# A transformer block in fp32 on one core: every SBUF tile gets another address

## The chip, the core and the metric

The kernel runs on one core of one Trainium2 chip. The time is that of the device, in microseconds; three runs of the kernel before gave 1016.59, 1017.27 and 1018.25 us (median 1017.27). The core's engines are TensorE (PE; its weight loads are listed as PEld), VectorE (DVE), ScalarE (ACT), GpSimd (POOL) and SyncE (SP), which here issues nearly all DMAs. SBUF is the core's working memory: 128 partitions, and every tile occupies the same byte range in each of them. Addresses below are such byte offsets within a partition, in units of 1024 bytes (K).

## The reference

One layer of a Conformer macaron block on 512 tokens of width 1024, in fp32:

```python
x = x + 0.5 * swiglu(rmsnorm(x, ffn1_norm), w_gate1, w_up1, w_down1)   # D_FF = 2816
proj = rmsnorm(x, mix_norm) @ w_in
out_a = chunked_relbias_attention(qa, ka, va, a_rel_bias)              # 8 heads of 64
out_b = mla_attention(c_q, c_kv, k_rope, ...)                          # 8 heads, q and k of 96
x = x + concatenate([out_a, out_b]) @ w_out
x = x + 0.5 * swiglu(rmsnorm(x, ffn2_norm), w_gate2, w_up2, w_down2)
x = rmsnorm(x, final_norm)

def swiglu(h, w_gate, w_up, w_down):
    return (silu(h @ w_gate) * (h @ w_up)) @ w_down
```

## The kernel before

Activations are held transposed, model or hidden dimension on the partitions and the 512 tokens along the row, so one tile of 128 rows by 512 fp32 takes 2K. Precision comes from splitting: each operand is a high part and a low part, and `mm3` (L150 to L153) makes each product of three matmuls: moving high on weights high, moving high on weights low, and moving low on weights high (their lines in the trace are L151, L153 and L152). A matmul of 512 columns has one stationary operand (128 by 128, loaded by a PEld instruction) and one moving operand of 512 columns, both read from SBUF.

The stages on PE, in order:

- FFN 1, gate and up (`gu`): for each of 22 hidden tiles two outputs of 8 x 3 matmuls, 1056 in all. Stationary: the split weights `whi`, `wlo`. Moving: the split input `xh`, `xl`.
- FFN 1, down (`dn`): 8 output tiles of 22 x 3 matmuls, 528 in all. Moving: the split hidden tiles `h1h`, `h1l`.
- Mixer: input projections (`pj`; here the weights move and `xh`, `xl` are stationary), then the attention of 16 heads.
- Output projection (`wo`, 192 matmuls; moving: `xh`, `xl`, which now hold the attention's output).
- FFN 2, gate and up (1056; moving: `x2h`, `x2l`), and down (moving: `h2h`, `h2l` for the first 14 hidden tiles, and `xh`, `xl`, used again, for the last 8). The last output tile is done in two halves of 256 columns.

`wunit` (L137 to L148) prepares weights: a DMA brings a block of 128 x 1024 into `raw`, ACT writes `whi` (L146) and POOL or DVE writes `wlo` (L147), four buffers each. `gate` (L156 to L168) makes a hidden tile from two finished PSUM banks on DVE, ACT and POOL.

The order on the engines comes from the recording layer's scheduler. The places of the tiles come from pools, which are stacked in the order of their opening: `const` (with `x`, `xh`, `xl`), `wpool` (`raw`, `whi`, `wlo`), `work`, `small`, and above them in turn the pools of the stages, `h1`, `mix` and `h2`, which use one range one after the other. A tile of a later stage waits until the instructions that use an older tile in its range are through. The addresses before, from the built program:

| tiles | before |
|---|---|
| x | 16.1K to 32.1K |
| xh, xl | 32.1K to 64.1K |
| raw | 69.4K to 85.4K |
| whi, wlo | 85.4K to 117.4K |
| work, small | 117.4K to 129.8K |
| h1h, h1l in turn | 129.8K to 217.8K |
| x2h, x2l, then h2h, h2l in turn | 129.8K to 217.8K |

In bytes, each tile of xh and xl begins 128 past a multiple of 512, each block of whi and wlo 384 past one, each tile of the h1 and h2 pools 256 past one.

Of the kernel before, what the change touches and what calls it, by code (L numbers as in the profile page):

```python
# [32 lines left out]
# columns of the packed parameter array  # L33
# [6 lines left out]
def tile_macaron_block(  # L40
# [20 lines left out]
    const = ctx.enter_context(tc.tile_pool(name="const", bufs=1))  # L61
    wpool = ctx.enter_context(tc.tile_pool(name="wpool", bufs=4))
    work = ctx.enter_context(tc.tile_pool(name="work", bufs=2))
    small = ctx.enter_context(tc.tile_pool(name="small", bufs=2))

# [1 line left out]
    x = [const.tile([P, S], F32, name=f"x{k}") for k in range(KD)]  # L67
    XH = [const.tile([P, S], F32R, name=f"xh{k}") for k in range(KD)]
    XL = [const.tile([P, S], F32R, name=f"xl{k}") for k in range(KD)]
    col = const.tile([P, NCOL], F32, name="col")  # L70
    raw0 = [wpool.tile([P, 1024], F32, tag="raw", name="raw") for _ in range(2)]
# [41 lines left out]
    def rsqrt(out, v, y, y2):  # L113
        """out = v^-1/2: by logarithm and exponential, then one Newton step."""
        act.activation(y, v, AF.Ln)
        act.activation(y, y, AF.Exp, scale=-0.5)
        dve.tensor_tensor(out=y2, in0=y, in1=y, op=ALU.mult)
        dve.tensor_tensor(out=y2, in0=y2, in1=v, op=ALU.mult)
        dve.tensor_scalar(out=y2, in0=y2, scalar1=-0.5, scalar2=1.5, op0=ALU.mult, op1=ALU.add)
        dve.tensor_tensor(out=out, in0=y, in1=y2, op=ALU.mult)  # L120

    def rstd_rows(ps):
        """rs[:, n] = (mean_d x[d, n]^2 + eps)^-1/2 on every partition."""
        sh = work.tile([P, S], F32R, tag="wa", name="sh")
        sl = work.tile([P, S], F32R, tag="wa", name="sl")
        act.copy(sh, ssum)
        dve.tensor_tensor(out=sl, in0=ssum, in1=sh.bitcast(F32), op=ALU.subtract)
        m = ps.tile([P, S], F32, tag="mm", name="ms")
        pe.matmul(m, lhsT=ones, rhs=sh, start=True, stop=False)
        pe.matmul(m, lhsT=ones, rhs=sl, start=False, stop=True)  # L130
        v = work.tile([P, S], F32, tag="wb", name="v")
        y = work.tile([P, S], F32, tag="wa", name="y")
        y2 = work.tile([P, S], F32, tag="wc", name="y2")
        dve.tensor_scalar(out=v, in0=m, scalar1=EPS, scalar2=None, op0=ALU.add)
        rsqrt(rs, v, y, y2)

    def wunit(src, n, lo_on=None, raw=None, step=1024):  # L137
        """A block of weights, split: hi + lo, both exact in 12 bits."""
        if raw is None:
            raw = wpool.tile([P, 1024], F32, tag="raw", name="raw")  # L140
            nc.sync.dma_start(out=raw[:, :n], in_=src)
        hi = wpool.tile([P, 1024], F32R, tag="whi", name="whi")
        lo = wpool.tile([P, 1024], F32R, tag="wlo", name="wlo")
        for c in range(0, n, step):
            cc = slice(c, min(n, c + step))
            act.copy(hi[:, cc], raw[:, cc])  # L146
            (lo_on or pool).tensor_tensor(out=lo[:, cc], in0=raw[:, cc], in1=hi[:, cc].bitcast(F32), op=ALU.subtract)  # L147
        return hi, lo  # L148
# [6 lines left out]
    def ffn(ps, gu, dn, H, XH, XL, after, raw0=None, squares=None, last=None):  # L155
        def gate(f, gup):  # L156
            """h = silu(g) u = (g / 2) (tanh(g / 2) + 1) u, split."""
            gs = work.tile([P, S], F32, tag="wa", name="gs")
            th = work.tile([P, S], F32, tag="wb", name="th")
            us = work.tile([P, S], F32, tag="wc", name="us")  # L160
            hh, hl = H[f]
            dve.tensor_tensor(out=gs, in0=gup[0], in1=rs, op=ALU.mult)  # L162
            act.activation(th, gs, AF.Tanh, scale=0.5)  # L163
            dve.scalar_tensor_tensor(out=us, in0=gup[1], scalar=0.5, in1=rs, op0=ALU.mult, op1=ALU.mult)  # L164
            dve.scalar_tensor_tensor(out=gs, in0=th, scalar=1.0, in1=gs, op0=ALU.add, op1=ALU.mult)  # L165
            pool.tensor_tensor(out=us, in0=us, in1=gs, op=ALU.mult)  # L166
            act.copy(hh, us)
            pool.tensor_tensor(out=hl, in0=us, in1=hh.bitcast(F32), op=ALU.subtract)  # L168
# [45 lines left out]
    # =====================================================  FFN 1  # L214
    with tc.tile_pool(name="h1", bufs=1, reuse_waits="tile") as hp, \
            tc.tile_pool(name="ps1", bufs=8, space=PSUM, reuse_waits="tile") as ps:
        H = [(hp.tile([P, S], F32R, name=f"h1h{f}"), hp.tile([P, S], F32R, name=f"h1l{f}")) for f in range(NF)]
        # the tensor engine's clock rises while the first loads are under way
        warm = ps.tile([P, S], F32, tag="mm", name="warm")
        dve.memset(H[0][0].bitcast(F32), 0.0)  # L220
        for _ in range(9):
            pe.matmul(warm, lhsT=H[0][0][:, 0:P], rhs=H[0][0], start=True, stop=True)

        for k in range(KD):
            split_x(k, C_FFN1)

        def squares():
            for k in range(KD):
                add_square(k, True)

        def after1(dt):
            split_x(dt, C_MIX)
            add_square(dt)

        ffn(ps, gu1, dn1, H, XH, XL, after1, raw0, squares)

    # =====================================================  mixer
    AH, AL = XH, XL
    with tc.tile_pool(name="mix", bufs=1, reuse_waits="tile") as mp:
        qA = mp.tile([P, NT, 512], F32, tag="qA", name="qA")  # L240
        kA = mp.tile([P, NT, 512], F32, tag="kA", name="kA")
        lat = mp.tile([P, NT, LAT], F32, tag="qB", name="lat")
        latT = mp.tile([P, 6, S], F32R, tag="vAh", name="latT")
        kB = mp.tile([P, NT, 512], F32, tag="kB", name="kB")
        VBh = mp.tile([P, NT, 4, 192], F32R, tag="vBh", name="VBh")
        VBl = mp.tile([P, NT, 4, 192], F32R, tag="vBl", name="VBl")
# [8 lines left out]
        # rtab[:, q/k, t, :]: cos*g1, sin*g2, sin*g1, cos*g2  # L255
# [11 lines left out]
        def factors(ss, n, width, scaled, name):  # L267
            """ss [P, NT, n] sums of squares -> factors of the RMS norm, rtok folded in where scaled."""
# [13 lines left out]
        def rope(dst, src, fac, i, n, tmp):  # L282
            """src [P, NT, n, 32] * fac -> normalised, rotated, into dst (gains in rtab)."""
# [13 lines left out]
        with tc.tile_pool(name="ps2", bufs=1, space=PSUM, reuse_waits="tile") as ps:  # L297
            NB = {"s": 2, "tr": 2, "t": 3, "pv": 1}

            def bank(group, i, name):  # L300
                """Bank i of one of the two groups of four."""
                tag = (("s",) * NB["s"] + ("tr",) * NB["tr"], ("t",) * NB["t"] + ("pv",) * NB["pv"])[group][i]
                return ps.tile([P, 512], F32, tag=tag, name=name, bufs=NB[tag])

            def in_proj(off, n, group):
                """The columns off.. of W_in for all tokens: four banks, one per token tile."""
# [10 lines left out]
            def sumsq(src, ss, nh, width):  # L317
                """ss[.., h] = sum of squares over each group of width columns of src."""
# [5 lines left out]
            # latents, with the token statistics  # L324
# [46 lines left out]
            # B: queries from their latents  # L371
# [25 lines left out]
            # B: keys and values from their latents  # L397
# [29 lines left out]
            def values_proj():  # L427
                """A: values."""
# [15 lines left out]
            def transposes(src):  # L444
                """The four token tiles of src(t) [128, n], transposed into one bank [n, 512]."""
# [13 lines left out]
            def front(h):  # L459
                """Transposed, scaled and split queries and keys of a head (A: of its pair)."""  # L460
# [37 lines left out]
            def softmax(qh, ql, kh, kl, bias):  # L498
                """Probabilities of the query tiles 3..0, on 128 (i + 1) keys each."""
                pa = wpool.tile([P, 1024], F32, tag="raw", name="pa")  # L500
                pb = wpool.tile([P, 1024], F32, tag="raw", name="pb")
# [18 lines left out]
            def flip(pi):  # L520
                """Probabilities with the keys on the partitions, split: keys 0 | keys 1 and keys 2 | keys 3."""
# [34 lines left out]
            # the stages of four neighbouring heads overlap  # L556
# [14 lines left out]
    # =====================================================  output projection, FFN 2, final norm  # L571
    with tc.tile_pool(name="h2", bufs=1, reuse_waits="tile") as hp, \
# [3 lines left out]
        H = [(hp.tile([P, S], F32R, name=f"h2h{f}"), hp.tile([P, S], F32R, name=f"h2l{f}")) for f in range(14)]  # L576
# [18 lines left out]
        # final norm: per half of the tokens, rstd as columns, spread over the partitions by the tensor engine  # L595
# [11 lines left out]
        def means(h):  # L607
            """The mean squares of these tokens in columns, with the last tile's part."""
# [46 lines left out]
def _kxm(w, kt, m):  # L655
    """[kt*128, m] -> [128, kt, m]: the rows of each k tile on the partitions."""
    return w.reshape(kt, P, m).transpose(1, 0, 2)
# [10 lines left out]
def _layout(i):  # L668
# [17 lines left out]
    # the bias of query p and key column c of a tile whose last 128 columns are the query's own block  # L686
# [34 lines left out]
```

## Time and profile before

| | before |
|---|---|
| three runs | 1016.59, 1017.27, 1018.25 us |
| profiled execution: span of its instructions (its whole time is not listed apart) | 1016.7 us |
| PE busy | 993.1 us, 98% |
| PE weight loads | 813.7 us, 80% |
| POOL, DVE, ACT busy | 591.5, 397.3, 387.6 us |
| HBM read | 87.02 MB, 88 GB/s over the span with the writes |

Matmuls overlap in this trace: one is listed with some 0.39 us from its start to its end, while the next starts after some 0.23 us. So the busy share says little of PE's pace; the distance from one matmul's start to the next one's, the pitch, says it. The profiled span lies 0.6 us below the median of the runs.

### The profile page before, as it was taken

The numbers are of one execution on the slowest core, as the hardware profiler recorded it, in microseconds if no ns is written. First come the engines' busy times: TensorE is split into PE (matmuls) and PEld (weight loads), VectorE is DVE, ScalarE is ACT, GpSimd is POOL, SyncE is SP. The second block draws the span as 40 slices with busy tenths as digits, with TensorE's granted clock in tenths as the row PEclk, the third lists the DMA queues.
The fourth block names the chain that finished last, engine by engine and source line by source line (L and its number), as shares of the span: only waits on it lengthen the run. The fifth ranks groups of instructions, "written<-read, shape, count | busy, mean of one in ns | idle before, by whom it ended". The sixth has DMA issues, their size and how long they took to land.

```text
span 1016.7 us, 12060 instructions
## 1 busy us (share of the span) xinstructions
PE 993.1 (98%) x4579; PEld 813.7 (80%) x4579; DVE 397.3 (39%) x687; ACT 387.6 (38%) x648; POOL 591.5 (58%) x429
## 2 busy tenths in 40 slices
PE   7999999999999999898999999999999999999996
PEld 4888888888888889786778978888888888888886
DVE  7534324323121224776788845143333332200002
ACT  4433323323222225663678853343232332222220
POOL 7586676676555521285355567586666656645540
PEclk7999999999999999998999999999999999999999
DMA  5423323323333333220010062323322332333302
GB/s 201 151 83 105 104 83 104 104 83 94 97 94 93 91 110 104 83 62 1 21 43 2 1 208 86 101 84 103 95 92 86 101 102 80 90 103 94 99 16 83
DMA packets 28714, 89.90 MB, mean 88 GB/s; under 512 B 3440, under 2 KB 5616, under 8 KB 28656
## 3 DMA queue, kind: packets, MB, share of 16 engines
q1 hardware_dynamic: 27504, 88.08, 27.8%
q10 hardware_dynamic: 1152, 1.05, 0.3%
q8 instruction: 36, 0.59, 0.2%
q14 instruction: 22, 0.18, 0.1%
HBM read 87.02 MB, written 2.10 MB: 88 GB/s over the span
## 4 chain that ended last, share of the span: by engine, by line
PE 88%; DVE 4%; POOL 2%; issue 2%; ACT 1%; DMA 1%; POOLq 0%; DVEq 0%; ACTq 0%; SPq 0%
PE gu L153 16%; PE gu L152 16%; PE gu L151 16%; PE dn L151 8%; PE dn L152 8%; PE dn L153 8%; PE pj L153 2%; PE pj L151 2%; PE pj L152 2%; PE wo L153 1%; PE wo L152 1%; PE wo L151 1%; PE t L533 1%; PE s L151 1%; PE tr L448 1%
## 5 line engine op out<-in xcount | busy, mean ns | idle before, releaser
L147 POOL TENSOR_TENSOR wlo<-raw,whi 128x1024 fp32r<-128x1024 f32 x138 | 323.3, 2344 | 159.3 <-ACT whi L146 159.3
L146 ACT CAST whi<-raw 128x1024 fp32r<-128x1024 f32 (+3 forms) x165 | 167.3, 1014 | 468.1 <-PE gu L152 263.6
L152 PE MATMUL gu<-xl,whi 128*128 128x512 f32 x352 | 139.2, 396 | 3.0 <-DVE xl L101 2.9
L151 PE MATMUL gu<-xh,whi 128*128 128x512 f32 x352 | 138.3, 393 | 1.5 <-ACT whi L146 1.5
L151 PE MATMUL gu<-x2h,whi 128*128 128x512 f32 x352 | 139.0, 395 | 0.0
L153 PE MATMUL gu<-x2h,wlo 128*128 128x512 f32 x352 | 138.9, 395 | 0.0
L152 PE MATMUL gu<-x2l,whi 128*128 128x512 f32 x352 | 138.9, 395 | 0.0
L153 PE MATMUL gu<-xh,wlo 128*128 128x512 f32 x352 | 138.4, 393 | 0.2 <-DVE wlo L147 0.2
L166 POOL TENSOR_TENSOR us<-us,gs 128x512 f32<-128x512 f32 x44 | 58.4, 1329 | 111.8 <-DVE us L164 110.0
L165 DVE SCALAR_TENSOR_TENSOR gs<-th,gs 128x512 f32<-128x512 f32 x44 | 90.1, 2052 | 31.7 <-ACT th L163 31.7
L162 DVE TENSOR_TENSOR gs<-gu,rs 128x512 f32<-128x512 f32 x44 | 30.4, 691 | 178.5 <-PE gu L153 171.3
L199 DVE SCALAR_TENSOR_TENSOR x<-dn,x 128x512 f32<-128x512 f32 (+1 forms) x17 | 11.2, 661 | 198.9 <-PE dn L153 198.9
L152 PEld LDWEIGHTS gu<-xl,whi 128*128 128x128 f32 x352 | 66.6, 189 | 20.3 <-DVE xl L101 7.0
L151 PEld LDWEIGHTS gu<-xh,whi 128*128 128x128 f32 x352 | 66.8, 190 | 15.9 <-ACT whi L146 1.9
L151 PEld LDWEIGHTS gu<-x2h,whi 128*128 128x128 f32 x352 | 66.1, 188 | 16.1
L152 PEld LDWEIGHTS gu<-x2l,whi 128*128 128x128 f32 x352 | 66.1, 188 | 16.1
L153 PEld LDWEIGHTS gu<-x2h,wlo 128*128 128x128 f32 x352 | 66.1, 188 | 16.0
L153 PEld LDWEIGHTS gu<-xh,wlo 128*128 128x128 f32 x352 | 66.8, 190 | 14.5 <-DVE wlo L147 1.1
L153 PE MATMUL dn<-h1h,wlo 128*128 128x512 f32 x176 | 69.5, 395 | 0.0
L151 PE MATMUL dn<-h1h,whi 128*128 128x512 f32 x176 | 69.5, 395 | 0.0
L152 PE MATMUL dn<-h1l,whi 128*128 128x512 f32 x176 | 69.5, 395 | 0.0
L164 DVE SCALAR_TENSOR_TENSOR us<-gu,rs 128x512 f32<-128x512 f32 x44 | 30.4, 690 | 69.0 <-PE gu L153 65.5
(318 smaller groups left out, 1830.4 us busy)
## 6 DMA issues: line engine op xcount, KB each, us to landing
raw<-in_gu SPq DMA_DIRECT2D x87, 512.0 KB, 3.6
raw<-in_dn SPq DMA_DIRECT2D x32, 512.0 KB, 3.5
raw<-in_dn SPq DMA_DIRECT2D x16, 384.0 KB, 3.1
raw<-in_w_in SPq DMA_DIRECT2D x12, 512.0 KB, 3.5
raw<-in_w_out SPq DMA_DIRECT2D x8, 512.0 KB, 4.2
x<-in_xT SPq DMA_DIRECT2D x8, 256.0 KB, 5.2
bias<-in_bias_tab SPq DMA_DIRECT2D x8, 256.0 KB, 2.7
raw<-in_w_in SPq DMA_DIRECT2D x4, 416.0 KB, 3.4
```

What stands on the lines that cost most here:

```text
L146: act.copy(hi[:, cc], raw[:, cc])
L147: (lo_on or pool).tensor_tensor(out=lo[:, cc], in0=raw[:, cc], in1=hi[:, cc].bitcast(F32), op=ALU.subtract)
L151: pe.matmul(out, lhsT=ah, rhs=bh, start=start, stop=False)
L152: pe.matmul(out, lhsT=ah, rhs=bl, start=False, stop=False)
L153: pe.matmul(out, lhsT=al, rhs=bh, start=False, stop=stop)
L162: dve.tensor_tensor(out=gs, in0=gup[0], in1=rs, op=ALU.mult)
L164: dve.scalar_tensor_tensor(out=us, in0=gup[1], scalar=0.5, in1=rs, op0=ALU.mult, op1=ALU.mult)
L165: dve.scalar_tensor_tensor(out=gs, in0=th, scalar=1.0, in1=gs, op0=ALU.add, op1=ALU.mult)
L166: pool.tensor_tensor(out=us, in0=us, in1=gs, op=ALU.mult)
L199: dve.scalar_tensor_tensor(out=x[dt][:, h], in0=pt[:, h], scalar=0.5, in1=x[dt][:, h], op0=ALU.mult, op1=ALU.add)
L448: pe.transpose(pt[0:src(t).shape[1], t * P:(t + 1) * P], src(t), ident)
L533: pe.transpose(tt[:, o + i * P:o + (i + 1) * P], pi[i][:, j * P:(j + 1) * P], ident)
```

## The change

All instructions and their order on each of the five engines stay the same, row for row. The pools get a side: `const`, `wraw` (a new pool, with `raw` alone), `work` and `small` are laid from the top of SBUF downward; `opers` (a new pool, with `xh` and `xl`), `wpool` (now `whi` and `wlo` alone) and the pools of the stages are laid from the bottom upward. In `h1` and `h2` all high parts now come before all low parts. In `mix` the tiles `latT` and `VBh` come first, then `qA`, `VBl`, `kA`. Comments are gone too, which shifts line numbers by 3 to 7.

```diff
-    const = ctx.enter_context(tc.tile_pool(name="const", bufs=1))
-    wpool = ctx.enter_context(tc.tile_pool(name="wpool", bufs=4))
-    work = ctx.enter_context(tc.tile_pool(name="work", bufs=2))
-    small = ctx.enter_context(tc.tile_pool(name="small", bufs=2))
+    const = ctx.enter_context(tc.tile_pool(name="const", bufs=1, side="right"))
+    wraw = ctx.enter_context(tc.tile_pool(name="wraw", bufs=4, side="right"))
+    work = ctx.enter_context(tc.tile_pool(name="work", bufs=2, side="right"))
+    small = ctx.enter_context(tc.tile_pool(name="small", bufs=2, side="right"))
+    opers = ctx.enter_context(tc.tile_pool(name="opers", bufs=1, side="left"))
+    wpool = ctx.enter_context(tc.tile_pool(name="wpool", bufs=4, side="left"))
...
-    XH = [const.tile([P, S], F32R, name=f"xh{k}") for k in range(KD)]
-    XL = [const.tile([P, S], F32R, name=f"xl{k}") for k in range(KD)]
+    XH = [opers.tile([P, S], F32R, name=f"xh{k}") for k in range(KD)]
+    XL = [opers.tile([P, S], F32R, name=f"xl{k}") for k in range(KD)]
...
-            raw = wpool.tile([P, 1024], F32, tag="raw", name="raw")
+            raw = wraw.tile([P, 1024], F32, tag="raw", name="raw")
...
-        H = [(hp.tile([P, S], F32R, name=f"h1h{f}"), hp.tile([P, S], F32R, name=f"h1l{f}")) for f in range(NF)]
+        HH = [hp.tile([P, S], F32R, name=f"h1h{f}") for f in range(NF)]
+        HL = [hp.tile([P, S], F32R, name=f"h1l{f}") for f in range(NF)]
+        H = list(zip(HH, HL))
...
+        latT = mp.tile([P, 6, S], F32R, tag="vAh", name="latT")
+        VBh = mp.tile([P, NT, 4, 192], F32R, tag="vBh", name="VBh")
         qA = mp.tile([P, NT, 512], F32, tag="qA", name="qA")
+        VBl = mp.tile([P, NT, 4, 192], F32R, tag="vBl", name="VBl")
         kA = mp.tile([P, NT, 512], F32, tag="kA", name="kA")
...
-        H = [(hp.tile([P, S], F32R, name=f"h2h{f}"), hp.tile([P, S], F32R, name=f"h2l{f}")) for f in range(14)]
+        HH = [hp.tile([P, S], F32R, name=f"h2h{f}") for f in range(14)]
+        HL = [hp.tile([P, S], F32R, name=f"h2l{f}") for f in range(14)]
+        H = list(zip(HH, HL))
```

The addresses after, from the built program:

| tiles | after |
|---|---|
| xh, xl | 16.1K to 48.1K |
| whi, wlo | 48.1K to 80.1K |
| h1h, then h1l | 80.1K to 124.1K, 124.1K to 168.1K |
| x2h, then x2l | 80.1K to 96.1K, 96.1K to 112.1K |
| h2h, then h2l | 112.1K to 140.1K, 140.1K to 168.1K |
| work, small | 174.3K to 186.7K |
| raw | 186.7K to 202.7K |
| x, constants | 202.7K to 223.9K |

Every tile that TensorE reads in the FFNs and the output projection now begins 128 bytes past a multiple of 512.

Because other old tiles now lie under the mixer's tiles, six waits at the end of FFN 1 are set anew. On POOL, between the last weight block of FFN 1 and the mixer's first products, before (VBh, VBl: values with their zero columns; kpe: rotary keys; rtmp: rotary tables):

```order
L111 TENSOR_TENSOR ssum<-ssum,sq 128x512 [waits Activation_49,Pool_49]
L249 MEMSET VBh 128x16x64 [waits PE_49]
L249 MEMSET VBl 128x16x64 [waits PE_49]
L250 MEMSET kpe 128x384 [waits PE_49]
L261 TENSOR_TENSOR rtmp<-ctab,rgain 128x4x16 [waits DMAHW6_49,DMAHW5_49,PE_49]
```

The same place on POOL after:

```order
L114 TENSOR_TENSOR ssum<-ssum,sq 128x512 [waits Activation_49,Pool_49]
L254 MEMSET VBh 128x16x64 [waits PE_49]
L254 MEMSET VBl 128x16x64 [waits PE_49]
L255 MEMSET kpe 128x384
L266 TENSOR_TENSOR rtmp<-ctab,rgain 128x4x16 [waits DMAHW6_49,DMAHW5_49]
```

No row has moved. Counted in PE's instructions, VBh waits for one 9 earlier and VBl for one 12 later, the last down matmul; kpe and rtmp, behind VBl, no longer name PE. On SP, at the same time, before (ctab, rgain: the rotary tables' inputs):

```order
L141 DMA raw<-in_w_in 128x1024 [waits DMAHW0_49,DVE_49]
L252 DMA ctab<-in_rope_tab 128x128 [waits PE_49]
L254 DMA rgain<-in_rope_gain 128x64
L472 DMA bias<-in_bias_tab 128x512 x2
L141 DMA raw<-in_w_in 128x1024 [waits DMAHW1_49,DVE_49]
```

The same place on SP after:

```order
L144 DMA raw<-in_w_in 128x1024 [waits DMAHW0_49,DVE_49]
L257 DMA ctab<-in_rope_tab 128x128 [waits PE_49]
L259 DMA rgain<-in_rope_gain 128x64 [waits PE_49]
L477 DMA bias<-in_bias_tab 128x512 x2
L144 DMA raw<-in_w_in 128x1024 [waits DMAHW1_49,DVE_49]
```

Again no row has moved; ctab waits for a matmul 13 earlier, and rgain for one 10 earlier than ctab waited for before.

## Rows read from the trace of the kernel before

**Rows 1.** The profile's page: span, busy time by engine, granted clock in 40 slices.

```profile
span 1016.7 us, 12060 instructions
...
PE 993.1 (98%) x4579; PEld 813.7 (80%) x4579; DVE 397.3 (39%) x687; ACT 387.6 (38%) x648; POOL 591.5 (58%) x429
...
PEclk7999999999999999998999999999999999999999
```

**Rows 2.** The page's chain that ended last, by engine.

```profile
PE 88%; DVE 4%; POOL 2%; issue 2%; ACT 1%; DMA 1%; POOLq 0%; DVEq 0%; ACTq 0%; SPq 0%
```

**Rows 3.** Waits over the span: who waited for whom, us, times, longest.

```profile
ACT whi L146 <- PE gu L152: 263.6, 85, 5.0
```

**Rows 4.** Timeline, PE, 100 to 140 us (start, duration): first and last matmul.

```profile
99.76 0.39 PE L153 MATMUL gu<-xh,wlo 128*128 128x512 f32 x1
...
139.88 0.39 PE L153 MATMUL gu<-xh,wlo 128*128 128x512 f32 x1
```

**Rows 5.** Timeline, PE, 700 to 740 us: first and last matmul.

```profile
699.69 0.40 PE L153 MATMUL gu<-x2h,wlo 128*128 128x512 f32 x1
...
739.82 0.40 PE L151 MATMUL gu<-x2h,whi 128*128 128x512 f32 x1
```

**Rows 6.** Timeline, PE, 280 to 320 us: first and last matmul.

```profile
279.74 0.39 PE L152 MATMUL dn<-h1l,whi 128*128 128x512 f32 x1
...
319.87 0.39 PE L153 MATMUL dn<-h1h,wlo 128*128 128x512 f32 x1
```

**Rows 7.** Timeline, PE, 404 to 418 us: first and last matmul.

```profile
403.81 0.39 PE L153 MATMUL pj<-whi,xl 128*128 128x512 f32 x1
...
417.86 0.39 PE L152 MATMUL pj<-wlo,xh 128*128 128x512 f32 x1
```

**Rows 8.** Windows 100:140 and 700:740: busy by engine (instructions), clock, DMA share, GB/s.

```profile
100.00:140.00 40.00, 40.00 (x178) 33.15 (x177) 13.99 (x11) 11.72 (x14) 26.26 (x15) 1.00 0.28 93
700.00:740.00 40.00, 40.00 (x173) 32.20 (x172) 13.85 (x11) 11.71 (x14) 25.22 (x15) 1.00 0.32 93
```

**Rows 9.** Timeline, PE, 891 to 898 us, around the last 24 matmuls of one output tile.

```profile
892.19 0.39 PE L153 MATMUL dn<-h2h,wlo 128*128 128x512 f32 x1
892.42 0.39 PE L151 MATMUL dn<-xh,whi 128*128 128x512 f32 x1
...
893.12 0.39 PE L151 MATMUL dn<-xh,whi 128*128 128x512 f32 x1
...
897.88 0.40 PE L151 MATMUL dn<-h2h,whi 128*128 128x512 f32 x1
```

**Rows 10.** Groups by line and shape, PE: xcount, busy us, mean ns, idle before.

```profile
L151 PE MATMUL gu<-x2h,whi 128*128 128x512 f32 x352 | 139.0, 395 | 0.0
...
L151 PE MATMUL dn<-h1h,whi 128*128 128x512 f32 x176 | 69.5, 395 | 0.0
...
L151 PE MATMUL dn<-h2h,whi 128*128 128x512 f32 x98 | 38.7, 395 | 0.0
...
L151 PE MATMUL wo<-xh,whi 128*128 128x512 f32 x64 | 24.9, 389 | 0.0
...
L151 PE MATMUL dn<-xh,whi 128*128 128x512 f32 x56 | 21.8, 389 | 0.0
```

**Rows 11.** Groups by line and shape, ACT and POOL.

```profile
L147 POOL TENSOR_TENSOR wlo<-raw,whi 128x1024 fp32r<-128x1024 f32 x122 | 293.9, 2410 | 116.6 <-ACT whi L146 116.6
...
L168 POOL TENSOR_TENSOR h1l<-us,h1h 128x512 fp32r<-128x512 f32 x22 | 28.6, 1298 | 0.0
...
L168 POOL TENSOR_TENSOR xl<-us,xh 128x512 fp32r<-128x512 f32 x8 | 10.4, 1297 | 0.0
```

**Rows 12.** Timeline, POOL, 372 to 386 us (in brackets: idle before, and what ended it).

```profile
376.32 0.95 POOL L249 MEMSET VBl<- 128x1024 f32 x1 [1.14 <-PE dn L153]
...
381.38 1.63 POOL L261 TENSOR_TENSOR rtmp<-ctab,rgain 128x64 f32<-128x64 f32 x5 [3.75 <-DMA rgain<-in_rope_gain]
```

**Rows 13.** Timeline, PE, 378.9 to 397.2 us: the mixer's first projection, and what follows it.

```profile
378.90 0.35 PE L151 MATMUL pj<-whi,xh 128*128 128x416 f32 x1
...
396.97 0.39 PE L328 MATMUL mt<-onec,ssum 128*128 128x1 f32 x3
```

More of the change, by code (lines that the diff above doesn't have):

```diff
@@ L59, in tile_macaron_block @@
     act, dve, pool, pe = nc.scalar, nc.vector, nc.gpsimd, nc.tensor
-    const = ctx.enter_context(tc.tile_pool(name="const", bufs=1))
-    wpool = ctx.enter_context(tc.tile_pool(name="wpool", bufs=4))
-    work = ctx.enter_context(tc.tile_pool(name="work", bufs=2))
-    small = ctx.enter_context(tc.tile_pool(name="small", bufs=2))
+    const = ctx.enter_context(tc.tile_pool(name="const", bufs=1, side="right"))
[4 more added lines that the diff above has]
+    wpool = ctx.enter_context(tc.tile_pool(name="wpool", bufs=4, side="left"))
     x = [const.tile([P, S], F32, name=f"x{k}") for k in range(KD)]
-    XH = [const.tile([P, S], F32R, name=f"xh{k}") for k in range(KD)]
-    XL = [const.tile([P, S], F32R, name=f"xl{k}") for k in range(KD)]
+    XH = [opers.tile([P, S], F32R, name=f"xh{k}") for k in range(KD)]
+    XL = [opers.tile([P, S], F32R, name=f"xl{k}") for k in range(KD)]
     col = const.tile([P, NCOL], F32, name="col")
-    raw0 = [wpool.tile([P, 1024], F32, tag="raw", name="raw") for _ in range(2)]
+    raw0 = [wraw.tile([P, 1024], F32, tag="raw", name="raw") for _ in range(2)]
     nc.sync.dma_start(out=x[0], in_=xT[0:P, :])
@@ L212, in ffn @@
             after(dt)
-    with tc.tile_pool(name="h1", bufs=1, reuse_waits="tile") as hp, \
+    with tc.tile_pool(name="h1", bufs=1, side="left", reuse_waits="tile") as hp, \
             tc.tile_pool(name="ps1", bufs=8, space=PSUM, reuse_waits="tile") as ps:
-        H = [(hp.tile([P, S], F32R, name=f"h1h{f}"), hp.tile([P, S], F32R, name=f"h1l{f}")) for f in range(NF)]
+        HH = [hp.tile([P, S], F32R, name=f"h1h{f}") for f in range(NF)]
+        HL = [hp.tile([P, S], F32R, name=f"h1l{f}") for f in range(NF)]
+        H = list(zip(HH, HL))
         warm = ps.tile([P, S], F32, tag="mm", name="warm")
@@ L238, in tile_macaron_block @@
     AH, AL = XH, XL
-    with tc.tile_pool(name="mix", bufs=1, reuse_waits="tile") as mp:
+    with tc.tile_pool(name="mix", bufs=1, side="left", reuse_waits="tile") as mp:
+        latT = mp.tile([P, 6, S], F32R, tag="vAh", name="latT")
+        VBh = mp.tile([P, NT, 4, 192], F32R, tag="vBh", name="VBh")
         qA = mp.tile([P, NT, 512], F32, tag="qA", name="qA")
+        VBl = mp.tile([P, NT, 4, 192], F32R, tag="vBl", name="VBl")
         kA = mp.tile([P, NT, 512], F32, tag="kA", name="kA")
         lat = mp.tile([P, NT, LAT], F32, tag="qB", name="lat")
-        latT = mp.tile([P, 6, S], F32R, tag="vAh", name="latT")
         kB = mp.tile([P, NT, 512], F32, tag="kB", name="kB")
-        VBh = mp.tile([P, NT, 4, 192], F32R, tag="vBh", name="VBh")
-        VBl = mp.tile([P, NT, 4, 192], F32R, tag="vBl", name="VBl")
         kpe = mp.tile([P, NT, QK], F32, tag="kpe", name="kpe")
@@ L498, in softmax @@
             def softmax(qh, ql, kh, kl, bias):
-                pa = wpool.tile([P, 1024], F32, tag="raw", name="pa")
-                pb = wpool.tile([P, 1024], F32, tag="raw", name="pb")
+                pa = wraw.tile([P, 1024], F32, tag="raw", name="pa")
+                pb = wraw.tile([P, 1024], F32, tag="raw", name="pb")
                 pi = [pb[:, 256:384], pb[:, 0:256], pa[:, 512:896], pa[:, 0:512]]
@@ L569, in tile_macaron_block @@
                     values(it - 1, seg.pop(it - 1))
-    with tc.tile_pool(name="h2", bufs=1, reuse_waits="tile") as hp, \
+    with tc.tile_pool(name="h2", bufs=1, side="left", reuse_waits="tile") as hp, \
             tc.tile_pool(name="ps4", bufs=7, space=PSUM, reuse_waits="tile") as ps:
```

## The prediction

> **What bounds the kernel.** I read the page first: TensorE is busy 98% of the 1016.7 us span, and its granted clock is at the full 2.4 GHz level in nearly every slice [rows 1]. The chain of waits gives PE 88% of the time [rows 2], and the longest wait on the chip is that of ACT, which splits the weights, for PE to free a buffer [rows 3]: the suppliers wait for TensorE, not the reverse. So the FFNs and the output projection take as long as their matmuls take, and what counts is the pitch from one start to the next. That I read from timelines, stage by stage, as last start less first start over the number of steps:
>
> - FFN 1 gate and up, moving xh and xl: 99.76 to 139.88 us in 177 steps, 226.7 ns [rows 4].
> - FFN 2 gate and up, moving x2h and x2l: 699.69 to 739.82 us in 172 steps, 233.3 ns [rows 5].
> - FFN 1 down, moving h1h and h1l: 279.74 to 319.87 us in 172 steps, 233.3 ns [rows 6].
> - Input projection, moving the weights: 403.81 to 417.86 us in 62 steps, 226.6 ns [rows 7].
>
> So there are two paces, 6.6 ns or 2.9% apart, and the same instruction stream runs at both: FFN 1 and FFN 2 gate and up differ in nothing but the moving tiles. Clock 1.00, some 93 GB/s of DMA and the work of DVE, ACT and POOL are alike in the two windows [rows 8], so neither the throttle nor other engines' traffic makes the difference. In FFN 2's down the pace changes with the operand inside one output tile: the last 24 matmuls, which move xh and xl, take from 892.42 to 897.88 us, 5.46 us or 227.5 ns each, between stretches on h2h and h2l at the slow pace [rows 9]. By the address tables, what moved fast lay below 117.4K, and what moved slowly lay above 129.8K. That is the fact the sum rests on.
>
> **The change part by part.** No instruction goes, comes or moves; the tiles move, and six waits are set anew.
>
> *FFN 2 gate and up.* x2h and x2l go from 129.8K-161.8K to 80.1K-112.1K, where the projection's moving weights ran at 226.6 ns [rows 7]. Three groups of 352, of which the row shows one: 1056 matmuls [rows 10]: 1056 x 6.6 ns = 7.0 us. The whole stage lies on PE's path, so all of it counts. Least 0, most 7.0.
>
> *FFN 1 down.* 3 x 176 = 528 matmuls [rows 10]. The high parts come to lie at 80.1K-124.1K, the low parts stay above 124.1K. In `mm3` two moving operands of three are high parts, so at most 352 x 6.6 ns = 2.3 us. But rows 9 show that pace does not change at once: the first three matmuls on xh and xl after the slow stretch still take 892.42 to 893.12 us, 0.70 us or 233 ns each. With a low part from the upper region in every group of three, the two others would hardly get out of that. I take 0.5 us, near the row's 0; both ends stay, 0 and 2.3 us (and 528 x 6.6 = 3.5 us if the border lies higher).
>
> *FFN 2 down.* 3 x 98 = 294 matmuls on h2h and h2l [rows 10]. Of 14 high parts 8 come below 128K; by the same reasoning 0.1 us, with ends 0 and 8/14 x 196 x 6.6 ns = 0.7 us. The 168 on xh and xl (3 x 56) are fast already. The last output tile, in halves of 256 columns, I count at nothing.
>
> *FFN 1 gate and up, output projection.* 1056 and 192 matmuls at 226.7 ns; xh, xl and the weights go lower still. Value 0; the other end is the slow rival below.
>
> *The mixer.* Here PE waits for others, so faster reads by PE gain nothing: 0, at most a few tenths. Whether DVE, ACT and POOL care for addresses the trace can say: POOL's low-part product takes 1298 ns into h1l above 129.8K and 1297 ns into xl below 64.1K [rows 11]. So moving `raw`, `work` and `x` to the top costs nothing there, and POOL, at 2.41 us for a weight block [rows 11] against 24 x 0.2267 = 5.4 us of matmuls on it, still keeps ahead at the fast pace.
>
> *The waits.* VBl's memset waits 12 PE instructions longer, 12 x 0.233 = 2.8 us, so it starts at about 379.1 instead of 376.32 us; behind it in POOL's queue stand kpe and rtmp, which started at 381.38 us, held by the DMA of rgain [rows 12]. That DMA, held behind ctab in SP's queue, may now go 10 instructions or 2.3 us earlier, and the two nearly cancel. Who waits for them is the rotation of the keys, after PE's first projection, which runs from 378.90 to 396.97 us [rows 13]: 18 us of cover. Without that cover it would be 2.8 us. Value 0.
>
> Sum: 7.0 + 0.5 + 0.1 = 7.6 us less than the profiled execution's 1016.7, so 1009.1 us; that execution lies 0.6 us below the median of the runs, 1017.27, which gives **1009.7 us**.
>
> **The rivals.**
>
> *1. It is not height but where tiles begin (faster still).* The tiles at 233 ns begin 256 bytes past a multiple of 512, those at 227 ns 128 or 384 past, as the weights do; the trace has no upper tile with the other start, so it cannot part the two. If the start against that of the weights decides, every moving tile of the FFNs becomes fast, the low parts too: 1878 x 6.6 ns = 12.4 us, so 1004.9. For it: the slow pace is the same at 130K and at 218K, and 128-byte steps are the only other thing that parts the groups. Against: nothing in the trace shows it by itself.
>
> *2. The stages at 227 ns lose their pace (slower).* In those stages the moving tile and the weights began 256 bytes apart modulo 512 (128 against 384). After the change they begin 0 apart, and xh, xl and the high weights stand within one stretch of 48K. If TensorE's reads of the two operands get on only at the old distance, FFN 1 gate and up, the output projection and the xh part of FFN 2 down fall to 233.3 ns: (1056 + 192 + 168) x 6.6 ns = 9.3 us, and nothing is gained elsewhere: 1026.6. It decides as soon as the first gate unit of FFN 1 after the change shows 233 ns. For it: there is no row at distance 0. Against: within a stage the weights' slices and buffers change their address all the time and the pace does not.
>
> *3. Addresses do not matter (no change).* The pace might belong to the stage, as the state it entered in, and not to the place: then 1017.3. Against it: in rows 9 the pace follows the operand within a tile, for each of seven output tiles. The Trainium skill's page "SBUF — State Buffer", section "Who interferes with whom", says that only the port pair shared by VectorE and GpSimd makes operands contend and that PE never waits on anyone; its page "TensorE: Matmul & The Clock Gate", section "Back-to-back issue gap", puts a 512-column matmul at 512/2.4 + 2.5 = 216 ns wherever its operand lies. By that rule this change is worth nothing. The trace disagrees with it: 226.7 and 233.3 ns at a granted clock of 1.00, and two paces where the rule has one.
>
> **How the numbers follow.** Forecast (lower is faster, with a border between 117K and 130K) 0.48, at 1009.7, its own range 1006 to 1011; rival 1 0.20, at 1004.9; rival 2 0.14, at 1026.6; rival 3 0.14, at 1017.3; 0.04 for a border so low that only part of x2 gains, 1012 to 1016. Two tenths of a per cent, 2.0 us, is about what this measurement can tell from no change. Faster by more than that: 0.48 + 0.20 + 0.03 = 0.71; within it 0.14; slower 0.15. The range must hold rivals 1 and 3 and leaves out rival 2: 1003 to 1018.5.
>
> **What would show it.** Right: the timeline at 700 us has a pitch of 226.7 ns, FFN 1's gate and up keeps it, and FFN 1's down stays near 232, with the pitch of the low parts above that of the high parts. Rival 1: the down stages run at 226.7 too. Rival 2: FFN 1 gate and up at 233. Rival 3: all pitches as before. The step most likely to be wrong is the down stages' 0.6 us, which may be 0 or 3. A mixer longer or shorter by over 1 us (378.90 us to the first output projection) would refute the zero on its waits.

## The result and the profile after

The changed kernel takes 1004.69 us (median of four runs, 1003.16 to 1006.24), the kernel before, run beside it, 1017.38 us: ratio 0.9877, 95% interval 0.9862 to 0.9892. It is 12.7 us shorter; the forecast had 7.6.

The profiled execution of the changed kernel took 1005.75 us, with a span of 1004.0; so a span leaves out some 1.75 us of an execution, and the span of 1016.7 before says nothing of whether that execution lay below the median. Its page, span, busy time and granted clock, against [rows 1]:

```profile
span 1004.0 us, 12060 instructions
...
PE 980.4 (98%) x4579; PEld 813.8 (81%) x4579; DVE 397.7 (40%) x687; ACT 387.3 (39%) x648; POOL 591.5 (59%) x429
...
PEclk8999999999999999999999999999999999999998
```

PE lost 12.7 us of busy time and the span lost 12.7; the other engines' work is what it was. Who waited for whom (us in total, times, longest), against [rows 3]:

```profile
ACT whi L149 <- PE gu L155: 258.0, 85, 5.9
```

So TensorE still sets the end. What changed is its pitch. Timelines of PE after (start, duration), first and last matmul of the stretches that answer to [rows 4], [rows 6] and [rows 5]:

```profile
99.71 0.39 PE L155 MATMUL gu<-xl,whi 128*128 128x512 f32 x1
...
139.83 0.39 PE L155 MATMUL gu<-xl,whi 128*128 128x512 f32 x1
...
279.69 0.39 PE L154 MATMUL dn<-h1h,whi 128*128 128x512 f32 x1
...
319.81 0.39 PE L154 MATMUL dn<-h1h,whi 128*128 128x512 f32 x1
...
699.78 0.39 PE L155 MATMUL gu<-x2l,whi 128*128 128x512 f32 x1
...
739.90 0.39 PE L155 MATMUL gu<-x2l,whi 128*128 128x512 f32 x1
```

Each stretch now holds 178 matmuls: 40.12 us / 177 = 226.7 ns in all three. Before, the last two had 173 matmuls in their 40 us, at 233.3 ns. The two windows of [rows 8] after (busy by engine with instructions, clock, DMA share, GB/s) have become alike in PE's counts:

```profile
100.00:140.00 40.00, 40.00 (x178) 33.14 (x177) 14.33 (x11) 12.19 (x15) 26.30 (x15) 1.00 0.29 99
700.00:740.00 40.00, 40.00 (x178) 33.13 (x177) 14.32 (x11) 12.19 (x15) 27.72 (x15) 1.00 0.28 93
```

Where the time went, by stage, as the distance from the first matmul of one stage to the first of the next, in the two profiled executions:

| stage | before, us | after, us | difference |
|---|---|---|---|
| up to the first gate/up matmul | 6.9 | 6.5 | -0.4 |
| FFN 1 gate and up | 248.80 | 250.03 | +1.2 |
| FFN 1 down | 123.19 | 119.68 | -3.5 |
| mixer | 213.32 | 211.93 | -1.4 |
| output projection | 43.55 | 43.54 | 0.0 |
| FFN 2 gate and up | 246.86 | 239.87 | -7.0 |
| FFN 2 down, first seven tiles | 106.73 | 104.72 | -2.0 |
| last output tile and end | 27.37 | 27.65 | +0.3 |

The three stages whose pitch fell give 12.5 us. FFN 1's gate and up and the mixer differ by about 1 us between kernels that start their tiles alike there too (below), and here nearly cancel.

### The profile page after: what moved, and what is told of

Read it like the earlier page. It is cut to its first block, busy times and chain, and to the rows that moved or that the text cites. A ratio compares the mean times of both kernels' runs of the same rounds, so it can differ in the third digit from the quotient of the medians.

```text
span 1004.0 us, 12060 instructions
## 1 busy us (share of the span) xinstructions
PE 980.4 (98%) x4579; PEld 813.8 (81%) x4579; DVE 397.7 (40%) x687; ACT 387.3 (39%) x648; POOL 591.5 (59%) x429
## 4 chain that ended last, share of the span: by engine, by line
PE 88%; DVE 4%; POOL 2%; issue 2%; DMA 2%; ACT 1%; SPq 0%; POOLq 0%; DVEq 0%; ACTq 0%
PE gu L155 16%; PE gu L156 16%; PE gu L154 16%; PE dn L156 8%; PE dn L154 8%; PE dn L155 8%; PE pj L156 2%; PE pj L154 2%; PE pj L155 2%; PE wo L154 1%; PE wo L156 1%; PE wo L155 1%; PE t L538 1%; PE s L154 1%; PE tr L453 1%
## 5 line engine op out<-in xcount | busy, mean ns | idle before, releaser
L149 ACT CAST whi<-raw 128x1024 fp32r<-128x1024 f32 (+3 forms) x165 | 166.9, 1012 | 456.5 <-PE gu L155 258.0
L154 PE MATMUL gu<-x2h,whi 128*128 128x512 f32 x352 | 136.9, 389 | 0.0
L155 PE MATMUL gu<-x2l,whi 128*128 128x512 f32 x352 | 136.8, 389 | 0.0
L156 PE MATMUL gu<-x2h,wlo 128*128 128x512 f32 x352 | 136.8, 389 | 0.0
```

Source lines behind the costliest of these rows:

```text
L154: pe.matmul(out, lhsT=ah, rhs=bh, start=start, stop=False)
L155: pe.matmul(out, lhsT=ah, rhs=bl, start=False, stop=False)
L156: pe.matmul(out, lhsT=al, rhs=bh, start=False, stop=stop)
```

## The experiments

At 226.7 ns two things had changed at once: the moving tiles lay lower, and they began at the same place as the weights, counted modulo 256 bytes. (Before, x began 128 and the weights 384 past a multiple of 512, so these two already agreed modulo 256, and x2, h1 and h2 stood 128 off.) Theory A: the agreement of starts counts. Theory H, the forecast's: the height counts. Theory M: the moving tile's own start counts, whatever that of the weights. All kernels keep every instruction; they shift tiles by small unused ones, some let scratch tiles of the mixer share a place to make room, and the last takes another order of tiles. "Distance" below is a moving tile's start less the weights' start, modulo 256. The first two were timed in rounds beside the kernel before (4 and 10 runs); the others ran once, with a profile.

**High, but aligned.** The kernel before, with 128 bytes ahead of h1 and of x2, nothing else:

```diff
+        hp.tile([P, 32], F32, name="pad1")    # first in pool h1
+        hp.tile([P, 32], F32, name="pad2")    # ahead of x2h
```

> The kernel before, with 128 unused bytes ahead of the tiles of the h1 and h2 pools: every tile stays at its height (129.8K to 218K), only its start goes from 256 to 384 past a multiple of 512, as the weights have it. Mixer untouched. Theory A (start of the moving tile against the start of the weights, modulo 256, decides): gate and up of FFN 2 and both down stages go from 233.3 to 226.7 ns, 1878 x 6.6 ns = 12.4 us less, about 1005. Theory H (height decides): nothing changes, 1017.4. Theory M (the moving tile's own start decides, a multiple of 256 being bad): as A, 1005.

Measured: 1004.42 us, ratio to before 0.9874 (0.9858 to 0.9891). Two unused tiles give all that the new layout gives (1004.69). Timeline of PE in this kernel, first and last matmul of 280 to 320 and of 700 to 740 us:

```profile
279.66 0.39 PE L153 MATMUL dn<-h1h,wlo 128*128 128x512 f32 x1
...
319.78 0.39 PE L153 MATMUL dn<-h1h,wlo 128*128 128x512 f32 x1
...
699.64 0.39 PE L152 MATMUL gu<-x2l,whi 128*128 128x512 f32 x1
...
739.99 0.39 PE L153 MATMUL gu<-x2h,wlo 128*128 128x512 f32 x1
```

40.12 us in 177 steps and 40.35 in 178: 226.7 ns, with h1 still from 129.8K to 217.8K. FFN 1 down took 119.68 us, FFN 2 gate and up 239.84, the first seven tiles of its down 104.72. Height is refuted; A and M both told this.

**Low, but 128 off.** The changed kernel with the same two tiles:

> The changed kernel, with 128 unused bytes ahead of the tiles of the h1 and h2 pools: they stay low (80K to 168K), but begin 256 past a multiple of 512, the weights and xh, xl 128 past. Theories A and M: gate and up of FFN 2 and both down stages fall back to 233.3 ns, 12.4 us more, about 1017. Theory H: no change, 1004.7.

Measured: 1016.89 us, ratio 0.9998 (0.9988 to 1.0007): the whole gain gone. PE, 700 to 740 us:

```profile
699.70 0.39 PE L154 MATMUL gu<-x2h,whi 128*128 128x512 f32 x1
...
739.83 0.39 PE L155 MATMUL gu<-x2l,whi 128*128 128x512 f32 x1
```

40.13 us in 172 steps, 233.3 ns, at 80K to 112K. A and M both told this run too; the next two kernels part them.

**Everything shifted by 128, or the weights alone.** In the changed kernel, 128 bytes ahead of all operands; then ahead of the weights, and 128 more ahead of h1, x2 and h2, which so keep their start modulo 256 while the weights lose theirs (in both, two of the mixer's `z` scratch tiles share a place to make room; the lines for h1 and h2 are as above):

```diff
+    opers.tile([P, 32], F32, name="pad0")                             # first kernel
...
+    wpool.tile([P, 32], F32, tag="pad0", name="pad0", bufs=1)         # second kernel
```

> The changed kernel, with 128 unused bytes at the bottom of the whole left stack: xh, xl, weights and all stage tiles begin 256 past a multiple of 512, so their distances to each other stay 0 (one 128-byte scratch tile of the mixer is shared to make room). Theory A: all stages keep 226.7 ns, 1004.7. Theory M: all 3294 matmuls of 512 columns in the FFNs and the output projection go to 233.3 ns, 21.7 us more, about 1026. Theory H: 1004.7.

> The changed kernel, with 128 unused bytes ahead of the weights and 128 more ahead of the tiles of h1 and h2: the weights begin 256 past a multiple of 512, xh and xl 128 past, the tiles of h1 and h2 384 past. Theory A: every stage with 512 columns is at 233.3 ns, also FFN 1 gate and up and the output projection, 3294 x 6.6 = 21.7 us more, about 1026. Theories M and H: 1004.7, all at 226.7 ns.

Measured: 1004.68 us with everything shifted, all stages at 226 to 227 ns; 1024.31 us with the weights alone off. PE in the first kernel from 700 to 740 us, then in the second from 100 to 140 us, in the first stage, where nothing but the weights has moved:

```profile
699.63 0.39 PE L157 MATMUL gu<-x2h,wlo 128*128 128x512 f32 x1
...
739.97 0.39 PE L155 MATMUL gu<-x2h,whi 128*128 128x512 f32 x1
...
99.64 0.39 PE L155 MATMUL gu<-xh,whi 128*128 128x512 f32 x1
...
139.85 0.40 PE L157 MATMUL gu<-xh,wlo 128*128 128x512 f32 x1
```

The first: 40.34 us in 178 steps, 226.6 ns. The second: 40.21 us in 173 steps, 232.4 ns; its FFN 1 gate and up took 255.96 us instead of 250.03, and the output projection 44.62 instead of 43.54. M falls twice, and H once more; A alone told all four kernels. These 232.4 ns are 0.9 below the 233.3 of the other kernels 128 off; why is open.

**Other distances.** Unused tiles of 32, 64 and 32 bytes ahead of h1, x2 and h2 in the changed kernel, so that h1 stands 32, x2 64 and h2 96 off; then of 160, 192 and 32 bytes, for 160, 192 and 224 off. Three readings of A: only the 128-byte half counts (A1), any distance costs the whole (A2), the cost grows with the distance (A3).

> The changed kernel with the stage tiles' starts moved by small steps against the weights: h1 by 32, x2 by 64, h2 by 96 bytes. How fine is theory A? A1 (only the 128-byte half of 256 bytes in which the start falls counts): all stay at 226.7 ns, 1004.7. A2 (any distance that is not a multiple of 256 costs the whole price): down 1, gate and up 2 and down 2 at 233 ns, 1017. A3 (the cost grows with the distance): 228, 230 and 232 ns, about 1010.

> As the run before, with h1 moved by 160, x2 by 192 and h2 by 224 bytes against the weights. A1: all three at 233 ns, 1017. A2: the same, 1017. A3 (distance to the nearest multiple of 256): 232, 230 and 228 ns, about 1010.

Measured: 1013.29 and 1017.72 us. The first one's x2, 64 off, 700 to 740 us:

```profile
699.69 0.39 PE L156 MATMUL gu<-x2h,wlo 128*128 128x512 f32 x1
...
739.98 0.39 PE L155 MATMUL gu<-x2l,whi 128*128 128x512 f32 x1
```

40.29 us in 176 steps, 228.9 ns. Mean pitches in ns by distance, over the stages of both kernels: 0: 226.7; 32: 233.3; 64: 228.9; 96: 233.7; 160: 234.3; 192: 233.3; 224: 233.3. So A1 and A3 fall, and A2 holds but for 64, which costs a third. It isn't symmetric: 192, which is 64 on the other side, costs the whole. Each of these distances was seen in one stage of one run only.

**Which operands must agree?** In the trace the next matmul's weight load (PEld) lies beside the running matmul: in the changed kernel a load of 0.19 us starts at 100.17 us, as the matmul ahead of it does. Theory O: each matmul's cost hangs on its own weights' start; theory L: on that of the weights loaded beside it. First all low moving parts stood 128 off, with high parts and weights aligned; then the low moving parts and the low weights both, so that moving and weights differed in two of three products.

> The changed kernel with the low parts of the moving operands alone (xl, h1l, x2l, h2l) 128 bytes off, high parts and both weights' parts as before; five scratch tiles of the mixer are shared to make room, so its own time is not compared. Of the three matmuls of each product one has a moving operand at odds with the weights. Theory L (a matmul is held up by the load of the next weights, which runs beside it, so its start counts against those) and theory O (against its own weights) both have one of three at odds: between 228.9 ns (6.6 ns on one of three) and 233 ns (the pace does not recover between) in all FFN stages.

> As the run before, with the low weights (wlo) 128 bytes off too. In the order of the program, high times high, low times high, high times low, each moving operand now agrees with the weights that are loaded while it streams (high, low, high), but two of three disagree with their own weights. Theory L: all FFN stages back at 226.7 ns, about 1004.7. Theory O: worse than the run before, 231 to 233 ns, 1018 to 1026.

Measured: 1018.64 and 1016.7 us, gate and up at 231.1 ns in both. Timeline of the second, 700 to 740 us:

```profile
699.83 0.40 PE L160 MATMUL gu<-x2h,wlo 128*128 128x512 f32 x1
...
739.81 0.40 PE L159 MATMUL gu<-x2l,whi 128*128 128x512 f32 x1
```

39.98 us in 173 steps, 231.1 ns. In FFN 1's down of the first, the product with the displaced operand is even the shortest step (low on high weights 229.6 ns, high on high 230.9, high on low 232.9), and all three are longer than 226.7: the cost of one disturbed product shows in the steps beside it too. Per group of three it is 13.3 ns over 3 x 226.7, two thirds of what three disturbed products cost, whether one product of the three differs or two. L falls, which had 226.7 ns for the second kernel. O has the second's pitch at the low end of its 231 to 233 ns, but not that it is no worse than the first's. The first kernel's output projection, with the same starts, ran at 233.3 ns; no theory tells why.

**The rest of the change.** The changed kernel with the old order inside its sides: high and low parts of h1 and h2 chunk by chunk in turn, the mixer's tiles as before.

```diff
-        HH = [hp.tile([P, S], F32R, name=f"h1h{f}") for f in range(NF)]
-        HL = [hp.tile([P, S], F32R, name=f"h1l{f}") for f in range(NF)]
-        H = list(zip(HH, HL))
+        H = [(hp.tile([P, S], F32R, name=f"h1h{f}"), hp.tile([P, S], F32R, name=f"h1l{f}")) for f in range(NF)]
```

> The changed kernel with the old order inside its two sides: the high and low parts of h1 and h2 lie chunk by chunk beside each other again instead of all highs and then all lows, and the mixer's tiles have their old order. All moving parts still start at the weights' place modulo 256 bytes. By the alignment of starts: no change, 1004.7 us within run-to-run 1.5 us, all 512-column stages at 226.7 ns, FFN1's down stage 119.7 us. By the height of addresses: the interleaved parts mix low and high addresses, and FFN1's down and FFN2's down stages lose half of what they won, 1007 to 1008 us, with pitches of 229 to 233 ns there. If the order of the mixer's tiles bore something of the gain, the mixer (211.9 us in the changed kernel) is longer than 213.3 us.

Measured: 1005.15 us, all 512-column stages at 226.7 ns, FFN 1 down 119.68 us, mixer 213.08. The order within the sides bears nothing of the gain. No kernel here had a median below 1004.4 us: 226.7 ns is the lowest pitch seen, and the 128-byte tiles reach it as well as the new layout.

## Why the prediction was right, and which step failed

The forecast of 1009.7 us was right in direction and within its range, but its mechanism was not the one at work. That it lies in the range is luck for the mechanism: 1003 to 1018.5 us was drawn to hold rivals 1 and 3 as well, and the sum's own range, 1006 to 1011, was missed. Point by point:

- *TensorE bounds the kernel, and pitch is what counts*: right. 12.5 of the 12.7 us are pitch times count in three stages.
- *FFN 2 gate and up, 7.0 us*: right in size, 246.86 to 239.87 us. The pitch fell to 226.7 ns as its row promised, but for another reason: with height refuted, this hit is luck.
- *FFN 1 down, 0.5 us*: wrong, 3.5 us. This is the failed step. "What moved fast lay below 117.4K, what moved slowly above 129.8K" is true of the trace of before, and was read as a cause; hence the low parts, still above 124K, were to hold the stage near 232 ns. The low parts ran at 227.0 ns, the high parts at 226.5, all of them at the fast pace. The bound of 3.5 us stood in the same paragraph for "a higher border"; what set it free was the start.
- *FFN 2 down, 0.1 us*: the same error, 2.0 us, over its upper end of 0.7. The prediction had called the two down stages its weakest step, "0 or 3"; they gave 5.5 us. After the change its pitch no longer follows the operand. PE around the 24 matmuls on xh and xl, against [rows 9]:

```profile
880.89 0.39 PE L156 MATMUL dn<-h2h,wlo 128*128 128x512 f32 x1
881.11 0.39 PE L154 MATMUL dn<-xh,whi 128*128 128x512 f32 x1
...
881.79 0.39 PE L154 MATMUL dn<-xh,whi 128*128 128x512 f32 x1
...
886.55 0.39 PE L154 MATMUL dn<-h2h,whi 128*128 128x512 f32 x1
```

The first three steps take 0.68 us and all 24 take 5.44: 226.7 ns from the first on, where before the first three still ran at 233.

- *Rival 1, starts against the weights, 1004.9 us at 0.20*: this was it, to 0.2 us. Its working, 1878 x 6.6 ns, needed no new number; only the chance was too small. The address table was as clear on starts as on height, and the forecast called them inseparable but gave height more than twice the chance. What spoke for starts was there: the same pace at 130K and at 218K, and a jump of 3% rather than a slope.
- *Rival 2, stages lose their pace at distance 0*: no, FFN 1 gate and up kept 226.7 ns.
- *Rival 3, addresses do not matter*: no. Where TensorE's own two operands begin cost 6.6 ns a matmul at 128 bytes off, and up to 7.6 at other distances, with other engines' work unchanged. The Trainium skill's page "SBUF — State Buffer", section "Who interferes with whom", has PE wait on no one. The runs disagree as far as TensorE's own two reads go: 226.7 against 233.3 ns by where they begin. The 216 ns that the prediction takes from the Trainium skill's page "TensorE: Matmul & The Clock Gate", section "Back-to-back issue gap", stand there for an isolated matmul; 226.7 ns was the lowest pitch of any run here.
- *The waits, 0*: right, but the test set for it was too narrow. POOL after, against [rows 12]:

```profile
376.47 0.95 POOL L254 MEMSET VBl<- 128x1024 f32 x1 [5.85 <-PE dn L156]
...
378.59 1.83 POOL L266 TENSOR_TENSOR rtmp<-ctab,rgain 128x64 f32<-128x64 f32 x5 [0.81 <-DMA rgain<-in_rope_gain]
```

And the first projection on PE, against [rows 13]:

```profile
376.25 0.35 PE L154 MATMUL pj<-whi,xh 128*128 128x416 f32 x1
...
394.30 0.95 PE L333 MATMUL mt<-onec,ssum 128*128 128x1 f32 x8
```

Against the projection's start, VBl's memset moved from 2.58 us ahead to 0.22 behind, the 2.8 us worked out; rtmp came 2.34 us behind it instead of 2.48; the projection took 18.05 us instead of 18.07. The mixer as a whole was 1.4 us shorter, over the 1 us that was to refute the zero. But the kernel before with its two small tiles, whose mixer layout is the old one, had 211.62 us, and the changed kernel with the old order of the mixer's tiles 213.08: that spread is there with either layout. Likewise FFN 1 gate and up, 250.03 us here, was 248.83 with the tiles of the second experiment and 248.86 in the last. Both spreads go with stretches at TensorE's lower clock level (a granted clock of 0.50, 1.2 GHz), whose place and length differ from execution to execution. In the mixer, after PE had been busy for only 0.84 us from 472 to 476 us, the clock stood at 0.50 from 476.0 to 482.8 us before, but only from 474.1 to 477.5 after; the 60 matmuls around it (470 to 489 us before) hold 0.9 of the 1.4 us. In FFN 1's first 96 matmuls, which hold the whole 1.2 us, it stood at 1.00 from 18.6 to 23.5 us before and at 0.50 after. No run sets the clock by itself, so this is read from the traces and not tested.
- *Moving `raw`, `work` and `x`, 0*: right. POOL's products take 2412 ns after for a weight block and 1294 ns into h1l, against 2410 and 1298 before [rows 11].
- *Slips in the working*: 1009.7 us is the median before less 7.6; the step to it from 1009.1 sets a span against whole times, which the result's 1.75 us show to be different things. The chances book 0.01 for 1012 to 1016 us as slower, where it belongs within 2.0 us of no change.

## What to carry to other kernels

Where TensorE sets the end, read its pitch stage by stage and operand by operand; two paces of one instruction stream are a cost to be found. Before moving a whole layout, compare where the moving and the stationary tiles begin, modulo 256 bytes: one unused tile of 128 bytes in each of two pools gave all of this change. And where two readings of an address table fit a trace equally, price both and don't let one of them take the chance without a row that parts them.

## What the runs showed of the hardware

Of matmuls with 512 fp32 columns the pitch was 226.7 ns where moving tile and weights began at the same place modulo 256 bytes, from 16K to 218K in SBUF, and 232 to 234 ns at all tested distances but 64 bytes (228.9 ns). Matmuls of 256 columns showed no cost: from the first of the 66 on the first half of the last output tile to the first on the second half took 7.91 us before (989.36 to 997.27) and the same after (976.31 to 984.23, to rounding), though h2 stood 128 off before. At some 120 ns a step something else may set their pace. Where in the chip the two streams meet, why 64 differs from 192, and why one displaced operand of three costs as much as two, stays open.
